# One attention and MLP layer in fp32: four small edits to the pipelined attention stage (a shared store buffer, an earlier weight load, a later place for short score columns, an earlier activation table load)

## The chip, the cores and the metric

The kernel runs on one core of a Trainium2 chip. The metric is the device time of one execution in microseconds (us), lower is better. A time that is shown is the median of several executions; the profile and the trace come from one further execution that the hardware profiler recorded.

Engines are named as the profile names them: PE is TensorE (its matmuls), PEld its weight loads, DVE is VectorE, ACT is ScalarE, POOL is GpSimd, SP is SyncE, which here issues nearly all DMAs. SPq and ACTq are the sequencers of SP and ACT, where their DMAs are issued.

## The reference

The layer has 2048 tokens and width 1024. It is an attention sub-layer and an MLP, each behind an RMS norm with shift, scale and gate from a conditioning vector. The attention has 16 heads of width 64 in two groups of eight.

```python
proj = h @ w_in[l]                          # 1024 -> 3072
q_sb, k_sb, v_sb, q_ca, k_ca, v_ca = jnp.split(proj, split_pts, axis=-1)
# group A, "stick-breaking", strictly causal:
w = jnp.where(strict, jnp.exp(log_beta + suffix), 0.0)   # suffix: cumulative sum of log(1 - beta)
# group B, chunked softmax over the own chunk of 64 and 8 chunks before it, with a relative bias:
p = jax.nn.softmax(s + bias, axis=-1)
mixed = jnp.concatenate([o_sb, o_ca], axis=-1)
x = x + gt1 * (mixed @ w_o[l])
x = x + gt2 * (jnp.square(jax.nn.relu(h2 @ w1[l])) @ w2[l])
```

## The kernel before, in words

Every fp32 product on PE is made of three matmuls on two fp32r halves ("hi" and "lo": `split`, a cast on ACT for hi and a subtraction on DVE or POOL for lo). Helpers record every PE, DVE, ACT and POOL instruction at one line (42), so that the profile's groups are told apart by the names of tiles. Tokens stand reversed, in four blocks of 512 (`TB`).

The program has three stages. Up to about 400 us the first stage projects blocks 3 and 2, and parts of 1 and 0, to queries, keys and values in scratch memory (`scr_q`, `scr_k`, `scr_v`). From about 400 to 1285 us the attention stage runs, which the change touches. From there to the end the MLP runs, and the trace shows it as matmuls `ps`.

**The attention stage** is one loop written out by hand (line 1303) over steps; four steps make a unit. A unit is one head and one block of queries, and for group A (class `SB`, `ca` 0) one block of keys as well; for group B (class `CA`, `ca` 1) it has a window of 640 keys for each 128 queries. Units come in this order: group A for query blocks 2 and 3, group B for 1, 2 and 3, group A for 1 and 0, group B for 0. So there are three turns from one group to the other (`turned`, line 1320). In one step the loop issues, in this order:

- for the unit two units back (`LAG` 8 steps): `transposes`, four PE transposes of finished weights into a PSUM bank `wt`;
- for the unit in front: `soft1` (group A: a sigmoid `z<-z` on ACT, a scan `p` on DVE and differences `b` on POOL; group B: bias added and minimum taken on DVE, `s<-cz` and `s<-ct`). At a turn it comes after the next item;
- `parts`: the split of `wt` into `wth` (ACT) and `wtl` (DVE), which frees its bank;
- `soft2` (group B: the exponential `e<-s` on ACT). At a turn it is the first exponential or sigmoid after the other kind, and ACT first loads a table (ACT_TABLE_LOAD);
- jobs of the step before (`done`): among them the sums and stores of finished heads;
- the value product `acc` of an older unit;
- `scores` for the next step (`z`, and `cz` in group B);
- `fill`: dense matmuls that have nothing to do with this unit, some six of 128x256 or three of 128x512 in a step (line 1344). A credit, which grows with the weight of each step, sets how many.

PE runs its instructions in this written order. The four PSUM banks of tag "z" are shared by `z`, `cz`, `ct` and `wt`; two banks of tag "ps" hold the dense work, and two hold `acc`.

**Short columns.** A row of group B has 640 scores and a bank 512. So 384 are made as `cz`, and the last 256 of two row blocks share one bank, `ct`. `ends(0)` makes it for row blocks 0 and 1 ahead of their first `cz`; `ends(2)` makes it for row blocks 2 and 3 in `scores` of row block 1, right behind that `cz`. DVE reads its part of `ct` one row block ahead (`tail`), behind `s<-cz` of the row block at hand.

**The dense work of the attention stage** is first the rest of the projection (`fill_qkv`, matmuls `pf`) for block 1 and then block 0, cut in pieces of 256 columns. A piece's weights are two halves of 1 MB (`fw`, four of the eight row groups each), in a ring of three buffers. While a piece runs, the halves of the next one are asked for in its second half of columns (`j` 1, line 1097). A piece of queries or keys has one pass over the eight row groups `k` there; a piece of values (4, 5, 10, 11) has two passes (`tt` 0 and 1), and both requests stand in the second: half 0 at `k` 0, and half 1 at `k` 4. Half 1 goes into the buffer of the running piece's half 0, whose last reader is `k` 3 of that second pass. After `fill_qkv` the dense work is the output projection (`outproj`, matmuls `po`, weights `ow`).

**Stores.** A piece's result is cast to `stf` or `svf` from pool `fp` (tag "st", three buffers), split, and stored by SP to `scr_q`, `scr_k` or `scr_v`. The output of two heads (`finish`, `total`, `keep`, lines 788 to 812) is added on POOL as `o`, cast by ACT to the hi half of `os`, subtracted on POOL to the lo half, and stored by SP to `scr_m`. `os` has one buffer of its own in pool `op` (line 806): the next cast to it waits until the store before has landed.

SP issues its DMAs in an order that the framework's scheduler sets; each waits in that queue for its own conditions, and what is behind it waits too.

Of the kernel before, what the change touches and what calls it, by code (L numbers as in the profile page):

```python
# [10 lines left out]
F32R = mybir.dt.float32r  # L11
BF16 = mybir.dt.bfloat16
AF = mybir.ActivationFunctionType
# [5 lines left out]
P = 128  # L19
# [6 lines left out]
TB = 512  # L26
# [53 lines left out]
def encoder_kernel(ctx, tc, xT, x3, wf, c, g1, g2, w_in, w_rest, gqk, bias, w_o, w1, w2, w_ada, b_ada, out):  # L80
    nc = tc.nc
    act, dve, pool, sp = nc.scalar, nc.vector, nc.gpsimd, nc.sync
# [35 lines left out]
    zero = cpool.tile([P, 1], F32, name="zero")  # L118
# [9 lines left out]
    cols = cpool.tile([P, 184], F32, name="cols")  # L128
# [116 lines left out]
    if True:  # L245
# [18 lines left out]
        behind = Later()  # L264
# [238 lines left out]
        act, dve, pool = (Ordered(tc, e) for e in (act, dve, pool))  # L503
# [130 lines left out]
        for k in range(KT):  # L634
            if k + 4 < KT:
                load_first(k + 4)
            j = k + 1
# [112 lines left out]
    ph = ctx.enter_context(ExitStack())  # L750
    if True:
# [51 lines left out]

        def keep(u, o):

            os = op.tile([P, 2, TB], F32R, tag="os", name=f"os{u.nm}", bufs=1)
            split(os[:, 0, :], os[:, 1, :], o, pool)
            q = act if u is units[-1] else sp
            q.dma_start(scr_m[u.g, u.ca * 4 + u.h // 2], os.bitcast(F32))
            pairs[u.g] += 1  # L810
            if pairs[u.g] == KT and u.g > 0:
                filler.append(Filler(outproj, u.g))
# [48 lines left out]
        class SB(Unit):  # L861
# [60 lines left out]
            def soft2(self, qi):  # L922
                pass

            def weights(self, qi, kb):
                w, c0 = self.ws[qi]
                return w[:, kb * P - c0 : (kb + 1) * P - c0]

        class CA(Unit):
# [39 lines left out]
            def scores(self, qi):  # L969
                nm = f"{self.nm}_{qi}"  # L970
                n, hn = self.size(qi)
                if qi == 0 and n > hn:
                    self.ends(0)
                self.z = z = pz.tile([P, TB], F32, tag="z", name=f"cz{nm}")
                ks = slice(qi * P, qi * P + hn)
                for l in range(2):
                    pe.matmul(z[:, :hn], self.q[:, l, qi * P : (qi + 1) * P], self.k[:, ks], start=l == 0, stop=l == 1)
                if qi == 1 and n > hn:
                    self.ends(2)

# [91 lines left out]
        def fill_qkv(self, tb, ht, pieces):  # L1072

            def load(piece, i):
                w = ring.tile([P, KT // 2, 2, CW], F32R, tag="r8", name=f"fw{tb}_{piece}_{i}")
                sp.dma_start(w.bitcast(F32), scr_w[piece,][:, i * 4 : i * 4 + 4, :, :])
                return w

            self.tiles = ht or []
            self.firsts = [lambda i=i: load(pieces[0], i) for i in range(2)]  # L1080
            yield None if ht else lambda k: scr_h[:, k]
            ht = self.moving()
            nxt = self.weights()
            yield "wait" if tb == 0 else "start"
            for n, piece in enumerate(pieces):
                grp, hf = divmod(piece, 2)
                w, nxt = nxt, []
                for j in range(2):
                    if n == len(pieces) - 1 and j:
                        yield "ahead"  # L1090
                    nm = f"f{tb}_{piece}_{j}"
                    ps = dense.tile([P, TB], F32, tag="ps", name=f"p{nm}")
                    last = 0 if grp < 2 else 1
                    for tt in range(last + 1):
                        tl = slice((2 * j + tt) * P, (2 * j + tt + 1) * P)
                        for k in range(KT):
                            if j and tt == last and k in (0, 4):
                                if n + 1 < len(pieces):
                                    nxt.append(load(pieces[n + 1], k // 4))
                                else:  # L1100
                                    yield "weight"
                            wk = w[k // 4][:, k % 4]
                            for i, (a, b) in enumerate(((0, 0), (0, 1), (1, 0))):
                                flags = {"start": k == 0 and i == 0, "stop": k == KT - 1 and i == 2}
                                if grp < 2:
                                    pe.matmul(ps, wk[:, a, j * P : (j + 1) * P], ht[k][:, b, :], **flags)
                                    yield 1.0
                                else:
                                    pe.matmul(ps[:, tt * CW : (tt + 1) * CW], ht[k][:, b, tl], wk[:, a, :], **flags)
                                    yield 0.5  # L1110

                    def keep(grp=grp, hf=hf, j=j, ps=ps, nm=nm, piece=piece):
                        if grp < 2:
                            st = fp.tile([P, 2, TB], F32R, tag="st", name=f"st{nm}")
                            src, hi, lo = ps, st[:, 0, :], st[:, 1, :]
                            home = scr_k[0, tb, hf * 2 + j].rearrange("l d t -> d l t") if grp else scr_q[0, tb, hf * 2 + j]
                        else:
                            st = fp.tile([P, 4, 2, 2, HD], F32R, tag="st", name=f"sv{nm}")
                            src, hi, lo = ps.rearrange("p (t h d) -> p h t d", t=2, d=HD), st[:, :, :, 0, :], st[:, :, :, 1, :]
                            home = scr_v[grp // 3, tb, hf][:, :, 2 * j : 2 * j + 2, :].rearrange("h p t e -> p h (t e)")  # L1120
                        act.copy(hi, src)

                        st2 = st if grp < 2 else st.rearrange("p h t l d -> p h (t l d)")

                        def rest(lo=lo, src=src, hi=hi, home=home, st2=st2, got=(piece, tb) if j else None):
                            dve.tensor_tensor(lo, src, hi.bitcast(F32), op=ALU.subtract)
                            sp.dma_start(home, st2.bitcast(F32))
                            if got:
                                have.add(got)

                        second.append(rest)

                    yield keep
# [146 lines left out]
        def value(u, j):  # L1280
            u.values(j)
# [14 lines left out]
        op = ph.enter_context(tc.tile_pool(name="op", bufs=2))  # L1296
        pado = ph.enter_context(tc.tile_pool(name="pado", bufs=1))
        pado.tile([P, 80], F32, tag="pad", name="pado")
        fp = ph.enter_context(tc.tile_pool(name="fp", bufs=3))
        wtp = ph.enter_context(tc.tile_pool(name="wtp", bufs=4))  # L1300
        ldq = sp
        steps = [(u, st) for u in units for st in range(STEPS)]
        for i in range(len(steps) + LAG):
            if i % STEPS == 0:
                if i // STEPS + AHEAD < len(units):
                    load(units[i // STEPS + AHEAD])
            vi = i - VST
            if vi >= 0 and vi % STEPS == 0 and vi // STEPS < len(units):
                units[vi // STEPS].load_values()
            front, fs = steps[i] if i < len(steps) else (None, 0)  # L1310
            back, bs = steps[i - LAG] if i >= LAG else (None, 0)
            done = list(soon)
            soon.clear()
            js = []
            if back is not None:
                nb = len(back.banks)
                js = range(nb * bs // STEPS, nb * (bs + 1) // STEPS)
            for j in js:
                back.transposes(j)
            turned = front is not None and i and front.ca != steps[i - 1][0].ca  # L1320
            if front is not None and not turned:
                front.soft1(fs)
            while first:
                first.pop(0)()
            while second:
                second.pop(0)()
            for j in js:
                back.parts(j)
                late.append((back, j))
            if turned:  # L1330
                front.soft1(fs)
            if front is not None:
                front.soft2(fs)
            for job in done:
                if turned:
                    later.add(3, job)
                else:
                    job()
            while len(late) > AVLAG:
                value(*late.pop(0))  # L1340
            if i + 1 < len(steps):
                u, st = steps[i + 1]
                u.scores(st)
            fill(front.weight if front else 0.6, 6 if turned else 0)
            later.tick()
        for u, j in late:
            value(u, j)
# [20 lines left out]
    if True:  # L1368
# [34 lines left out]
        steps, jobs = [], {}  # L1403
# [346 lines left out]
        for mb in (1, 0):  # L1750
            begin = len(steps)
            steps += [First(mb, j, i) for j in range(NP) for i in PRODUCTS]
            for j in range(NP):
                f = steps[begin + 7 * j]
# [124 lines left out]
```

## Time and profile before

| what | before |
|---|---|
| median of 3 executions | 2567.85 us (2565.67 to 2570.01) |
| the profiled execution's own time | 2574.0 us |
| span of the profile | 2572.2 us |
| granted TensorE clock, mean | 0.999 |
| PE busy | 2553.0 us, 12851 matmuls |
| weight loads busy (PEld) | 2155.4 us |
| DVE, ACT, POOL busy | 1867.0, 1394.8, 903.1 us |
| moved by DMA | 633.90 MB, mean 246 GB/s |
| ACT_TABLE_LOAD | 4 of 1.28 us |
| `os` casts and stores to `scr_m` | 32 |

PE is the engine that the others feed. Its busy time leaves 19.2 us of the span, start and end included. Matmuls are pipelined and their ends are modelled, so that a stretch that shows PE busy may still hold some slack; the idle times that the trace puts ahead of an instruction, with their releasers, are the safer reading. A wait is named after what ended last. The clock granted to TensorE is given for any stretch: at 1.00 a matmul of 512 columns takes its normal time, at 0.50 twice that.

### The profile page before, as it was taken

The page shows a single profiled execution, that of the slowest core. Times are in us where ns is not written, and L with a number is a line of the kernel's source. Part 1 is how long each engine was busy: PE and PEld are TensorE (multiplying, and loading weights), DVE is VectorE, ACT ScalarE, POOL GpSimd, SP SyncE. Part 2 cuts the span into 40 slices and gives each one's busy share as a digit, 9 for nine tenths or more (in the row PEclk, how much of TensorE's full clock was granted, in tenths as well). Part 3 has the DMA queues.
Part 4 walks back from the last instruction along what each step waited for, and adds up shares of the span by engine and source line. Part 5 has one row for each costly group of instructions (what it writes and reads, how often), then busy time and mean ns, then how long its engine had stood idle before and what let it go on. Part 6 is the DMA issues. An engine that isn't in the chain of part 4 may idle for free.

```text
span 2572.2 us, 39216 instructions
## 1 busy us (share of the span) xinstructions
PE 2553.0 (99%) x12851; PEld 2155.4 (84%) x12851; DVE 1867.0 (73%) x3102; ACT 1394.8 (54%) x2596; POOL 903.1 (35%) x1232
## 2 busy tenths in 40 slices
PE   9999999999999999999999999999999999999999
PEld 7888888888988988888978888888888888888887
DVE  7656767787778899898687777768766655645655
ACT  7323434668886666666754444556444545544443
POOL 4330244667666666666513333000003323100000
PEclk9999999999999999999999999999999999999999
DMA  9879887788887685766787767966764343465574
GB/s 394 341 283 371 316 321 255 227 271 262 251 249 259 210 280 191 241 196 217 233 331 260 268 249 285 329 234 223 254 239 149 140 168 144 157 241 196 200 270 152
DMA packets 251263, 633.90 MB, mean 246 GB/s; under 512 B 28209, under 2 KB 56881, under 8 KB 241202
## 3 DMA queue, kind: packets, MB, share of 16 engines
q1 hardware_dynamic: 249760, 626.67, 70.5%
q10 hardware_dynamic: 1298, 4.72, 0.4%
q8 instruction: 101, 1.65, 0.3%
q14 instruction: 104, 0.85, 0.1%
HBM read 439.92 MB, written 191.37 MB: 245 GB/s over the span
## 4 chain that ended last, share of the span: by engine, by line
PE 91%; DVE 3%; DMA 2%; ACT 2%; issue 1%; POOL 1%; SPq 0%; ACTq 0%; DVEq 0%; POOLq 0%
PE ps L42 47%; PE pt L42 11%; PE acc L42 7%; PE wt L42 6%; PE pf L42 5%; PE z L42 5%; PE po L42 4%; PE pq L42 3%; PE cz L42 2%; PE ct L42 1%; DVE p L42 1%; DMA scr_m<-os 1%; PE px L42 1%; POOL b L42 0%; DVE h L42 0%
## 5 line engine op out<-in xcount | busy, mean ns | idle before, releaser
L42 PE MATMUL ps<-oph,opv 128*128 128x512 f32 x2688 | 611.9, 390 | 0.2
L42 PE MATMUL ps<-h,opw 128*128 128x512 f32 x2664 | 604.2, 389 | 0.0
L42 PEld LDWEIGHTS ps<-oph,opv 128*128 128x128 f32 x2688 | 504.1, 188 | 106.0 <-DVE opv L42 0.8
L42 PEld LDWEIGHTS ps<-h,opw 128*128 128x128 f32 x2664 | 500.3, 188 | 103.6
L42 POOL TENSOR_TENSOR b<-p 128x512 f32<-128x512 f32 (+1 forms) x320 | 292.0, 912 | 207.2 <-DVE p L42 122.4
L42 ACT CAST wth<-wt 128x512 fp32r<-128x512 f32 (+1 forms) x432 | 244.0, 567 | 173.2 <-PE wt L42 169.0
L42 DVE TENSOR_TENSOR wtl<-wt,wth 128x512 fp32r<-128x512 f32 (+1 forms) x432 | 280.4, 653 | 66.8 <-ACT wth L42 65.3
L42 DVE TENSOR_TENSOR oph<-hw,oph 128x512 fp32r<-128x512 f32 x224 | 156.8, 700 | 211.8 <-ACT oph L42 211.8
L42 ACT CAST oph<-hw 128x512 fp32r<-128x512 f32 x224 | 139.3, 622 | 275.4 <-PE ps L42 273.7
L42 PE MATMUL pt<-w,ht 128*128 128x512 f32 x1248 | 288.0, 391 | 0.0
L42 POOL TENSOR_TENSOR ts<-w 128x512 f32<-128x512 f32 x32 | 46.5, 1452 | 660.4 <-DMA w<-in_w_dram 512.2
L42 PEld LDWEIGHTS pt<-w,ht 128*128 128x128 f32 x1248 | 233.1, 188 | 47.4
L42 DVE TENSOR_TENSOR_SCAN p<-z,p,zero 128x512 f32<-128x512 f32 x192 | 245.7, 1281 | 34.4 <-ACT z L42 23.8
L42 PE MATMUL acc<-wth,v 128*128 128x512 f32 (+3 forms) x544 | 218.0, 405 | 0.0
L42 ACT ACTIVATE z<-z 128x512 f32<-128x512 f32 (+1 forms) x320 | 165.9, 520 | 63.6 <-PE z L42 59.6
L42 PE MATMUL z<-k,q 128*128 128x512 f32 (+3 forms) x640 | 184.5, 370 | 2.3 <-DVE p L42 2.0
L42 PE MATMUL acc<-wtl,v 128*128 128x512 f32 (+3 forms) x544 | 181.7, 348 | 0.0
L42 DVE TENSOR_TENSOR opw<-w,opw 128x512 fp32r<-128x512 f32 x127 | 96.9, 765 | 113.2 <-ACT opw L42 113.1
L42 POOL TENSOR_TENSOR e<-e,cols 128x640 f32<-128x640 f32 (+1 forms) x128 | 142.8, 1120 | 86.7 <-DVE cols L42 73.0
L42 PE MATMUL wt<-ident,b 128*128 128x128 f32 x1088 | 166.7, 273 | 3.6 <-DVE p L42 3.0
L42 PE MATMUL po<-fx,ow 128*128 128x512 f32 x576 | 162.0, 393 | 0.0
L42 PEld LDWEIGHTS wt<-ident,b 128*128 128x128 f32 x1088 | 133.1, 141 | 30.7 <-DVE p L42 3.4
(200 smaller groups left out, 4085.5 us busy)
## 6 DMA issues: line engine op xcount, KB each, us to landing
hw<-scr_hid SPq DMA_DIRECT2D x112, 512.0 KB, 3.7
q<-scr_q SPq DMA_DIRECT2D x128, 256.0 KB, 4.5
w<-in_w_dram SPq DMA_DIRECT2D x64, 512.0 KB, 5.4
hw<-scr_s SPq DMA_DIRECT2D x64, 512.0 KB, 4.6
fw<-scr_w SPq DMA_DIRECT2D x28, 1024.0 KB, 6.7
k<-scr_k SPq DMA_DIRECT2D x224, 128.0 KB, 4.0
v<-scr_v SPq DMA_DIRECT2D x112, 256.0 KB, 4.1
wa<-in_w_ada_dram SPq DMA_DIRECT2D x48, 512.0 KB, 7.9
```

Source lines behind the costliest of these rows:

```text
L42: return lambda *x, **y: self.tc.keep_in_program_order(f(*x, **y))
```

## The change

Four edits, all in the attention stage:

1. `keep` takes `os` from pool `fp`, tag "st", which gets four buffers in place of three; the buffer of its own in `op` goes. The memory used is the same. `os`, `stf` and `svf` now take their buffers in turn from one ring.
2. The call `ends(2)` moves from `scores` into a new method `behind`, which the loop calls after `fill`. So the second `ct` of a unit stands behind that step's dense matmuls. Group A has an empty `behind`.
3. In `fill_qkv` half 0 of the next piece's weights is asked for at `k` 0 of the first pass (`tt` 0) and no more of the last; half 1 stays at `k` 4 of the last pass. For pieces of queries and keys, whose only pass is both, nothing changes.
4. At a turn the loop issues a one-column activation (into a column of `cols` that nothing reads) with the function that the front unit will need, ahead of `parts`. ACT's table load so comes ahead of the casts `wth` and no more behind them.

```diff
         def keep(u, o):
 
-            os = op.tile([P, 2, TB], F32R, tag="os", name=f"os{u.nm}", bufs=1)
+            os = fp.tile([P, 2, TB], F32R, tag="st", name=f"os{u.nm}")
             split(os[:, 0, :], os[:, 1, :], o, pool)
...
+            def behind(self, qi):
+                pass
+
...
                     pe.matmul(z[:, :hn], self.q[:, l, qi * P : (qi + 1) * P], self.k[:, ks], start=l == 0, stop=l == 1)
+
+            def behind(self, qi):
+                n, hn = self.size(qi)
                 if qi == 1 and n > hn:
                     self.ends(2)
...
-                            if j and tt == last and k in (0, 4):
+                            if j and (tt, k) in ((0, 0), (last, 4)):
                                 if n + 1 < len(pieces):
                                     nxt.append(load(pieces[n + 1], k // 4))
...
-        fp = ph.enter_context(tc.tile_pool(name="fp", bufs=3))
+        fp = ph.enter_context(tc.tile_pool(name="fp", bufs=4))
...
+            if turned:
+                act.activation(cols[:, 1:2], zero, AF.Exp if front.ca else AF.Sigmoid)
             for j in js:
                 back.parts(j)
...
             fill(front.weight if front else 0.6, 6 if turned else 0)
+            if i + 1 < len(steps):
+                u.behind(st)
             later.tick()
```

What moves is shown at three places. The first is SP's queue in the dense work of block 0, between pieces 4 and 5 of the values. `fw_5_1` is half 1 of piece 5, `fw_10_0` half 0 of piece 10, `svf_4_1` a result of piece 4, and `xr` are rows of the input. Before:

```order
L236 DMA xr_2_11577<-in_xT_dram 128x512
L778 DMA k_2_1_2_9819<-scr_k_2_1_117 64x512 x2
L785 DMA v_2_1_2_10087<-scr_v_2_0_144 128x512
L1076 DMA fw_5_1_9813<-scr_w_225 128x2048
L1076 DMA fw_10_0_10215<-scr_w_230 128x2048
L778 DMA k_2_1_3_9920<-scr_k_3_1_121 64x512
L1127 DMA scr_v_0_0_140<-svf_4_1_9876 128x4x256
```

After:

```order
L236 DMA xr_2_11579<-in_xT_dram 128x512
L778 DMA k_2_1_2_9821<-scr_k_2_1_117 64x512 x2
L785 DMA v_2_1_2_10089<-scr_v_2_0_144 128x512
L1082 DMA fw_5_1_9815<-scr_w_225 128x2048
L1082 DMA fw_10_0_10137<-scr_w_230 128x2048
L778 DMA k_2_1_3_9922<-scr_k_3_1_121 64x512
L1133 DMA scr_v_0_0_140<-svf_4_1_9878 128x4x256
```

Nothing moved here: `fw_10_0` is asked for sooner in the program (the last number in a name counts up with the program's order, 10215 and 10137), and stands at the same place in the queue. Elsewhere half 0 of piece 11 of block 1, of piece 2 of block 1 and of piece 11 of block 0 moved ahead by one to three rows of SP's queue.

The second is PE at the third turn, in the first unit of group B for query block 0 (head 0). `cz_0_0_1` are the scores of row block 1, `ct_0_0_2` the short columns of row blocks 2 and 3, and `po` the dense work. Before:

```order
L42 MATMUL cz_0_0_1_15145<-k_0_0_14895,q_0_0_14892 128x384 x2
L42 MATMUL ct_0_0_2_15148<-k_0_0_14895,q_0_0_14892 128x256 x4
L42 MATMUL po_0_15081<-fx_3_14829,ow_0_14564 128x512 x3
L42 MATMUL po_0_15081<-fx_4_15043,ow_0_14564 128x512 x3
L42 MATMUL po_0_15081<-fx_5_15045,ow_0_14564 128x512 x3
L42 MATMUL wt_7_0_2_1_15162<-ident,b_7_0_2_0_14902 128x128
```

After:

```order
L42 MATMUL cz_0_0_1_15147<-k_0_0_14897,q_0_0_14894 128x384 x2
L42 MATMUL po_0_15083<-fx_3_14831,ow_0_14566 128x512 x3
L42 MATMUL po_0_15083<-fx_4_15045,ow_0_14566 128x512 x3
L42 MATMUL po_0_15083<-fx_5_15047,ow_0_14566 128x512 x3
L42 MATMUL ct_0_0_2_15160<-k_0_0_14897,q_0_0_14894 128x256 x4
L42 MATMUL wt_7_0_2_1_15165<-ident,b_7_0_2_0_14904 128x128
```

`ct_0_0_2` moved behind nine dense matmuls. In 22 of the 24 units of group B it moved so, most often behind three; in two (head 0 of block 1, at the first turn, and head 1 of block 0) no dense matmul stands in that step and nothing moved.

The third is ACT at the first turn, from group A to B. `wth_7_2_2_2` and `wth_7_2_3_0` are casts of two steps, and `e_0_1_0` is the first exponential. Before:

```order
L42 ACTIVATE z_7_3_3_3_6264<-z_7_3_3_3_6264 128x128
L42 CAST wth_7_2_2_2_6278<-wt_7_2_2_2_6269 128x256
L42 CAST wth_7_2_3_0_6302<-wt_7_2_3_0_6297 128x512
L42 ACT_TABLE_LOAD
L42 ACTIVATE e_0_1_0_6311,cols<-s_0_1_0_6306,cols 128x640
```

After:

```order
L42 ACTIVATE z_7_3_3_3_6264<-z_7_3_3_3_6264 128x128
L42 CAST wth_7_2_2_2_6278<-wt_7_2_2_2_6269 128x256
L42 ACT_TABLE_LOAD
L42 ACTIVATE cols<-zero 128x1
L42 CAST wth_7_2_3_0_6303<-wt_7_2_3_0_6297 128x512
L42 ACTIVATE e_0_1_0_6312,cols<-s_0_1_0_6307,cols 128x640
```

The load and a one-column activation moved ahead of the cast; the other two turns change in the same way. On DVE and POOL no instruction moved.

## Prediction

> **What bounds the kernel now.** I read the page's totals first, then PE's own waits in the attention stage (400 to 1285 us), and then the timeline around the longest of them. The page says how little there is to win.
>
> ```profile
> span 2572.2 us, 39216 instructions
> ...
> PE 2553.0 (99%) x12851; PEld 2155.4 (84%) x12851; DVE 1867.0 (73%) x3102; ACT 1394.8 (54%) x2596; POOL 903.1 (35%) x1232
> ```
>
> PE is busy in all but 19.2 us. No edit takes a matmul away, so the change can return only what PE waits, and what its clock loses behind a wait. PE's waits in the attention stage, with total, count and longest:
>
> ```profile
> PE wt L42 <- DVE p L42: 3.0, 1, 3.0
> PE pf L42 <- DMA fw<-scr_w: 2.2, 1, 2.2
> PE z L42 <- DVE p L42: 2.0, 6, 0.6
> PE ct L42 <- DVE wtl L42: 1.3, 2, 0.6
> PE wt L42 <- DVE cols L42: 0.3, 1, 0.3
> PE wt L42 <- DVE wtl L42: 0.2, 1, 0.2
> PE ct L42 <- DVE cols L42: 0.2, 1, 0.2
> ```
>
> They sum to 9.2 us, and two single waits hold most. I call them A (3.0) and B (2.2), and the change speaks to both.
>
> **Wait A, edit 1.** The chain of waits has one store in it, shown from its issue to its landing:
>
> ```profile
> 462.94 8.29 DMA scr_m<-os
> ```
>
> The view of the line that issues these stores gives all 31 that SP issues:
>
> ```profile
> DMA to landing us min/median/max: 2.6/3.0/8.3
> ```
>
> ACT's, DVE's and PE's rows there (start, duration, and at the end the idle time before, with its releaser):
>
> ```profile
> 471.31 0.62 ACT L42 CAST os<-o 128x512 fp32r<-128x512 f32 x1 [4.52 <-DMA scr_m<-os]
> 471.83 0.58 ACT L42 CAST svf<-pf 128x512 fp32r<-128x512 f32 x1
> 472.31 1.07 ACT L42 ACTIVATE z<-z 128x512 f32<-128x512 f32 x2
> ```
>
> ```profile
> 473.00 1.28 DVE L42 TENSOR_TENSOR_SCAN p<-z,p,zero 128x512 f32<-128x512 f32 x1 [5.50 <-ACT z L42]
> ```
>
> ```profile
> 470.52 0.84 PE L42 MATMUL pf<-ht,fw 128*128 128x512 f32 x3
> 474.34 0.66 PE L42 MATMUL wt<-ident,b 128*128 128x128 f32 x4 [2.98 <-DVE p L42]
> ...
> 476.11 1.22 PE L42 MATMUL z<-k,q 128*128 128x512 f32 x2 [0.65 <-DVE p L42]
> ```
>
> The second of two `os` casts finds the only buffer still in flight to memory. ACT stands for 4.52 us, and the sigmoids `z` queue behind it; DVE's scan comes late, and PE waits for the bank that the scan frees: 2.98, then 0.65 us. The clock falls behind it, and behind B as well (window, then busy time of PE, PEld, DVE, ACT, POOL, then granted clock, DMA share, GB/s):
>
> ```profile
> 476.40:479.80 3.40, 3.40 (x10) 2.68 (x10) 3.40 (x5) 0.95 (x2) 2.19 (x5) 0.54 0.86 258
> 810.90:814.30 3.40, 3.40 (x16) 3.31 (x15) 1.65 (x2) 2.15 (x5) 0.14 (x1) 0.54 0.72 220
> ```
>
> At 0.54 for 3.40 us, 0.46 x 3.40 = 1.6 us of PE's work are lost. A costs 2.98 + 0.65 + 1.6 = 5.2 us.
>
> With a ring of four the cast needs only `o`, which POOL ends about 467.06:
>
> ```profile
> 465.77 1.29 POOL L42 TENSOR_TENSOR o<-o,otmp 128x512 f32<-128x512 f32 x1
> ```
>
> It starts at 467.1 in place of 471.31, 4.2 us sooner, and so do the `svf` cast, the sigmoids and the scan. PE's bank is then free at 474.34 - 4.2 = 470.1, while PE comes to it at 471.36 (470.52 + 0.84): 1.2 us to spare, so the whole stall goes. What is late next there are weights: half 1 of the running piece, 1 MB. It was issued ahead of that store in the same queue, so that I put its landing no later than the store's, 462.94 + 8.29 = 471.23; PE wants it in its next step, behind a `wt`, an `acc` and a `z`, about 1 us after 471.36 (an estimate). I take -5.2. The bound on the other side, if that cover fails, is 0.
>
> [...] Wait B stopped PE for 2.20 us, and the clock stood at 0.54 afterwards. [...]
>
> **Wait B, edit 3: 0.** The chain shows one weight transfer, and PE the place where it was missed:
>
> ```profile
> 800.13 9.34 DMA fw<-scr_w
> ```
>
> ```profile
> 804.58 1.34 PE L42 MATMUL pf<-fw,fx 128*128 128x256 f32 x10
> ...
> 806.91 0.40 PE L42 MATMUL pf<-fw,fx 128*128 128x256 f32 x2
> 809.51 0.73 PE L42 MATMUL pf<-fw,fx 128*128 128x256 f32 x4 [2.20 <-DMA fw<-scr_w]
> ```
>
> Ten and two matmuls are the twelve of `k` 0 to 3 (three each), which use half 0 of piece 5. The next uses half 1, `fw_5_1`. That half is asked for at `k` 4 before and after, because its buffer is free only when `k` 3 of piece 4 has been read; the edit asks sooner for half 0 alone, which was in time. In SP's queue `fw_5_1` and `fw_10_0` stand where they stood, with the same conditions. So B stays, 2.20 + 1.6 = 3.8 us, and the edit gives 0. The three rows of `fw` that do move in SP's queue are issued ahead of query, value and `scr_m` transfers, none of which is a releaser in PE's waits above; bounds 0 and one more wait like B, +3.8, and I take 0, as the list of waits has it.
>
> **Short columns, edit 2.** `ct` waited twice for `wtl` and once for `cols` (rows above), first here, at the first turn:
>
> ```profile
> 567.93 0.74 PE L42 MATMUL ct<-k,q 128*128 128x256 f32 x4 [0.64 <-DVE wtl L42]
> ```
>
> At this turn nothing moves, and 0.64 stays. The other, 1.3 - 0.6 = 0.7, is at the third turn; nine dense matmuls now stand ahead of it there; three of them take 0.86 us (next rows), so nine outlast the wait, and it goes. With the 0.2 at a moved `ct`, -0.9. Against it, DVE reads `ct` later. A plain step of group B shows how much it bears:
>
> ```profile
> 601.18 0.65 PE L42 MATMUL ct<-k,q 128*128 128x256 f32 x4
> 601.67 0.86 PE L42 MATMUL pf<-ht,fw 128*128 128x512 f32 x3
> ```
>
> ```profile
> 602.26 0.42 DVE L42 CUSTOM_DVE_ANT_0 s<-ct,bias 128x256 f32<-128x256 f32 x1
> ...
> 603.67 0.69 DVE L42 TENSOR_TENSOR wtl<-wt,wth 128x512 fp32r<-128x512 f32 x1 [0.91 <-ACT wth L42]
> ```
>
> `ct` ends at 601.83. The pair ends at 602.53 in either order, so that `ct` behind the three dense ones ends 0.70 later. DVE, which reads it at 602.26, comes 0.27 late; `wtl` had 0.91 idle ahead of it: covered.
>
> **Tables, edit 4.** A turn's rows on ACT, first turn and second:
>
> ```profile
> 566.57 0.59 ACT L42 CAST wth<-wt 128x512 fp32r<-128x512 f32 x1 [1.60 <-PE wt L42]
> 568.96 1.28 ACT L42 ACT_TABLE_LOAD   x1 [1.80 <-DVE cols L42]
> ```
>
> ```profile
> 762.24 0.58 ACT L42 CAST wth<-wt 128x512 fp32r<-128x512 f32 x1
> 762.84 1.28 ACT L42 ACT_TABLE_LOAD   x1
> 764.13 0.97 ACT L42 ACTIVATE z<-z 128x512 f32<-128x512 f32 x2
> ```
>
> The nearest row for the new one-column activation, from the groups of ACT (busy time, mean ns):
>
> ```profile
> L42 ACT ACTIVATE aff<-mod,gcol 128x1 f32<-128x1 f32 x8 | 3.1, 386 | 5.6 <-DVE mod L42 5.6
> ```
>
> Its cost lies between 0 and that 0.39. At the first turn ACT has 1.60 us free ahead of the cast, and load and activation take 1.28 to 1.67: they fit but for 0.07 us, the exponential comes 1.28 sooner, and PE was not waiting for it: 0. At the second there is no wait ahead of the cast: it moves by up to 1.67 us and the sigmoids by up to 0.39, while the six extra dense matmuls that a turn is given cover PE. Bounds 0 and +0.4; I take +0.2. The third is like the first: 0.
>
> [...]
>
> **Sum.** -5.2 - 0.9 + 0.2 + 0 = -5.9 us, from 2574.0 for the profiled execution to 2568.1. That execution is 6.15 above the median of the runs, 2567.85, and 4.0 above the slowest. I apply the difference to the median: **2562.0**. A measurement of this kernel can tell about 0.2% from no change, here 5.1 us (2562.7), so the forecast lies just beyond it.
>
> **The rivals.**
>
> *The store is quicker in timed runs.* A needs a landing over 8.29 - 3.6 = 4.7 us after the issue, and the median is 3.0. That timed runs are 4 to 8 us faster than the profiled one speaks for it; that the store is issued behind 1 MB of weights in the same queue, in every execution, against. Gain 0.7: 2567.2. Chance 0.15, no change.
>
> *Both waits go.* If edit 3 reaches B after all (less traffic beside `fw_5_1`), -5.9 - 3.8 = -9.7: 2558.2. The unmoved rows speak against; B's margin of only 2.2 us, for. Chance 0.13, faster.
>
> *The clock falls anyway.* The half clock has another cause than PE's gaps: -5.9 + 1.6 = -4.3, 2563.6. Both falls stand right behind the two longest gaps, which speaks against. Chance 0.07, no change.
>
> *Late short columns hold DVE.* In group B, at 22 places, if DVE's read of `ct` comes over 0.91 us late, `wtl` is late, the bank is not free, and PE waits up to the 0.70 by which `ct` moved: 22 x 0.70 = 15.4. With A gone and no gain on `ct`: -5.2 + 0.2 + 15.4 = +10.4, 2578.3; it ends slower from 0.46 us a place on. The 0.27 worked out above speaks against. Chance 0.08, slower.
>
> *The shared ring makes casts wait.* A cast of `stf` or `os` waits when the store four buffers back has not landed: 5.2 us a time by A's price. It takes three to end slower (-5.9 + 15.6 = +9.7, 2577.5). Against it: the longest landing of `os` is 8.3 us, and four more casts would have to come within it, where the stretch at A shows two. Chance 0.05, slower.
>
> **How the numbers follow.** The forecast has 0.52; its own range is 2559.6 to 2565.3 (-6.1 to -4.8 by the bounds of edits 2 and 4, and the 2.2 us by which the timed runs lie around their median), with 0.33 of it beyond 2562.7. Faster: 0.33 + 0.13 = 0.46. Same: 0.19 + 0.15 + 0.07 = 0.41. Slower: 0.13. The range reaches from 2558.2 - 2.2 = 2556.0 to 2567.2 + 2.2 = 2569.4; the slower cases are left out.
>
> **What would show it.** Right: no ACT wait of `os` on a store; the clock at 1.00 around 470 to 480; PE's wait for `fw` still there near 800, with its half clock; `ct` waits of 0.6 in all, at the first turn alone; three table loads ahead of casts. Wrong: a gap of PE near 470 all the same, B gone, `wtl` or `ct` with a wait in many steps of group B, or `stf` and `os` waiting for stores.

## The result, and the profile after

| | before | after |
|---|---|---|
| median of 22 executions each, in turns on one chip | 2569.94 us (2563.97 to 2577.32) | 2564.64 us (2562.45 to 2568.85) |
| ratio after to before | | 0.9985, 95% interval 0.9978 to 0.9991 |
| the profiled execution, its span | 2574.0, 2572.2 us | 2562.64, 2560.9 us |
| granted TensorE clock, mean | 0.999 | 1.000 |

The change is faster by 0.15% (0.09 to 0.22%), that is 3.9 us (2.3 to 5.7). The forecast was 5.9 us. The medians lie 5.3 us apart. The gain is under the 0.2% (5.1 us) that the prediction took as the least that can be told from no change; with 22 executions each the interval still leaves out 1.

The profiled executions lie 11.4 us apart, twice as far as the medians. The page of after:

```profile
span 2560.9 us, 39227 instructions
...
PE 2548.6 (100%) x12851; PEld 2153.9 (84%) x12851; DVE 1866.3 (73%) x3102; ACT 1396.2 (55%) x2599; POOL 903.4 (35%) x1232
```

PE's waits in the attention stage of after (400 to 1285 us; total, count, longest):

```profile
PE z L42 <- DVE p L42: 1.7, 5, 0.6
PE ct L42 <- DVE wtl L42: 0.6, 1, 0.6
PE wt L42 <- DVE cols L42: 0.3, 1, 0.3
PE wt L42 <- DVE wtl L42: 0.2, 1, 0.2
```

PE's idle time fell from 19.2 to 12.3 us, and its busy time by 4.4 us, of which 3.2 are, by the prediction's estimate, the two half clocks of before. The waits sum to 2.8 us where before had 9.2. A is gone, `ct` waits at the first turn alone, and **B is gone too**, against the forecast.

The place of A on ACT in after, and the landings of all `os` stores that SP issues:

```profile
467.40 0.62 ACT L42 CAST os<-o 128x512 fp32r<-128x512 f32 x1 [0.31 <-POOL o L42]
467.92 0.58 ACT L42 CAST svf<-pf 128x512 fp32r<-128x512 f32 x1
468.40 1.07 ACT L42 ACTIVATE z<-z 128x512 f32<-128x512 f32 x2
...
DMA to landing us min/median/max: 2.6/2.9/6.8
```

The cast waits for POOL's `o` alone. It starts 4.15 us after the first store was issued (463.25); the forecast had 467.1 against 462.94, 4.16 us. The store still took 6.8 us to land, and nobody waits for it. The windows there (window, busy time of PE, PEld, DVE, ACT, POOL, clock, DMA share, GB/s) show PE full and the clock at 1.00:

```profile
469.90:473.30 3.40, 3.40 (x19) 2.84 (x18) 3.40 (x5) 1.98 (x4) 2.40 (x5) 1.00 0.75 281
473.30:476.70 3.40, 3.40 (x20) 2.83 (x19) 3.40 (x5) 2.48 (x6) 2.19 (x5) 1.00 0.99 291
```

At the first turn ACT has the table load ahead of the cast:

```profile
559.35 0.38 ACT L42 CAST wth<-wt 128x256 fp32r<-128x256 f32 x1 [0.53 <-PE wt L42]
559.74 1.28 ACT L42 ACT_TABLE_LOAD   x1
561.03 0.20 ACT L42 ACTIVATE cols<-zero 128x1 f32<-128x1 f32 x1
561.31 0.59 ACT L42 CAST wth<-wt 128x512 fp32r<-128x512 f32 x1
563.72 0.83 ACT L42 ACTIVATE e<-s,cols 128x640 f32<-128x640 f32 x1 [1.82 <-DVE cols L42]
```

The one-column activation took 0.20 us (forecast 0 to 0.39). The exponential starts as soon as DVE's columns are there, with no load in between, and PE, which was not waiting for it, gains nothing, as forecast. At the place of B, half 1 of piece 5 landed sooner than in before (9.3); its issue in after (count, size, us to landing):

```profile
fw<-scr_w SPq DMA_DIRECT2D x1, 1024.0 KB, 6.9
```

SP issues the same rows around it at the same distances in both traces (`fw` 1.05 us behind `v` in each, and 5.37 and 5.34 us behind `scr_m`), so no edit had moved this transfer. That was the open question, together with the size: which edit gave the 3.9 us, and what took B away?

### The profile page after: what moved, and what is told of

It is laid out like the page before. It is cut to its first block, busy times and chain, and to the rows that moved or that the text cites. A ratio compares the mean times of both kernels' runs of the same rounds, so it can differ in the third digit from the quotient of the medians.

```text
span 2560.9 us, 39227 instructions
## 1 busy us (share of the span) xinstructions
PE 2548.6 (100%) x12851; PEld 2153.9 (84%) x12851; DVE 1866.3 (73%) x3102; ACT 1396.2 (55%) x2599; POOL 903.4 (35%) x1232
## 4 chain that ended last, share of the span: by engine, by line
PE 92%; DVE 3%; ACT 1%; DMA 1%; issue 1%; POOL 1%; SPq 0%; DVEq 0%; ACTq 0%; POOLq 0%
PE ps L42 46%; PE pt L42 11%; PE acc L42 7%; PE wt L42 7%; PE pf L42 6%; PE z L42 5%; PE po L42 4%; PE pq L42 3%; PE cz L42 2%; PE ct L42 1%; DVE p L42 1%; DVE h L42 1%; PE px L42 1%; POOL b L42 0%; DVE cy L42 0%
## 5 line engine op out<-in xcount | busy, mean ns | idle before, releaser
L42 DVE TENSOR_TENSOR opv<-hw,opv 128x512 fp32r<-128x512 f32 x224 | 155.8, 695 | 0.0
```

Source lines behind the costliest of these rows:

```text
L42: return lambda *x, **y: self.tc.keep_in_program_order(f(*x, **y))
```

## The experiments

Each was timed in turns with the kernel before, whose executions the kernels of one group share. Every edit not named is as in the kernel it starts from. The last column counts executions of 2568 us and more; I chose that limit after seeing the runs, because those of before fall into two heaps there (their medians are 2566.05 and 2570.55).

| kernel | edits in | median us | ratio to before, 95% | at or over 2568 |
|---|---|---|---|---|
| before, four groups together | none | | | 54 of 116 |
| after | 1, 2, 3, 4 | 2564.64 | 0.9985 (0.9978 to 0.9991) | 2 of 22 |
| e1_ring | 1 | 2565.28 | 0.9993 (0.9984 to 1.0001) | 1 of 11 |
| e2_ct | 2 | 2567.95 | 0.9995 (0.9985 to 1.0005) | 4 of 11 |
| e3_weights | 3 | 2567.59 | 1.0000 (0.9990 to 1.0009) | 5 of 11 |
| e4_table | 4 | 2566.50 | 1.0001 (0.9991 to 1.0010) | 4 of 12 |
| store_first | none, two DMAs exchanged | 2565.30 | 0.9989 (0.9980 to 0.9997) | 0 of 11 |
| heavy_before | none, more stored | 2569.42 | 1.0009 (0.9997 to 1.0021) | 10 of 12 |
| heavy_after | all, more stored | 2563.40 | 0.9983 (0.9972 to 0.9993) | 0 of 12 |
| ring3 | all, ring of 3 | 2564.06 | 0.9985 (0.9976 to 0.9994) | 1 of 11 |
| late6 | all, half 1 asked later | 2562.82 | 0.9983 (0.9973 to 0.9992) | 0 of 10 |
| halves | all, other order of `k` | 2563.51 | 0.9984 (0.9976 to 0.9993) | 2 of 11 |
| late_order | all, other order of `k` | 2563.96 | 0.9985 (0.9974 to 0.9996) | 0 of 10 |

### Each edit alone

The parts of the diff are those of the change. Edit 1 (e1_ring):

> Edit 1 alone (os in a ring of four with the other stores; weights, ct and tables as before). My theory, the store is what ACT waits for: no row of ACT waits for scr_m<-os, PE has no gap near 470 us and the clock stands at 1.00 there; the time falls by 3 to 5.2 us (a ratio of 0.9980 to 0.9988), nearly all that the whole change gave. PE's ct waits stay at 1.3 to 1.5 us. PE's wait for fw near 800 is there only when that half of the weights lands later than 7.2 us after its issue (9.34 less the 2.20 that PE waited). Rival, the store is quick in timed runs: at most -0.7 us, a ratio of 0.9997 or more, and the gain of the whole change comes from another edit.

ACT's cast near A, and the landing of the store before it (issued at 464.55):

```profile
468.71 0.62 ACT L42 CAST os<-o 128x512 fp32r<-128x512 f32 x1 [0.31 <-POOL o L42]
...
scr_m<-os SPq DMA_DIRECT2D x1, 512.0 KB, 8.7
```

The store was as late as in before (8.7 against 8.3 us), and the wait is gone all the same. The time fell by 2.8 us by the medians and 1.8 by the ratio, with an interval that reaches zero: less than forecast. Ten of eleven executions are under 2568 us.

Edit 2 (e2_ct):

> Edit 2 alone (the second pair of short columns behind the dense matmuls). My theory: PE's ct waits go from 1.5 us in all to 0.6 at the first turn alone; the time falls by 0 to 0.9 us, a ratio of 0.9996 to 1.0000. ACT's wait for the os store and PE's gap near 470 are there if that store lands later than 4.7 us. Rival, the late ct holds DVE: up to 0.70 us at 22 places, +15.4 us and a ratio of 1.006, with PE waits behind wtl in many steps between 570 and 760 us.

```profile
PE ct L42 <- DVE wtl L42: 0.6, 1, 0.6
```

That is the whole of PE's waits at `ct`, 0.6 us at the first turn, as forecast. No wait behind `wtl` came up in group B. The ratio is close to the 0.9996 that 0.9 us would give, and cannot be told from 1. This kernel has the single `os` buffer, and in its trace A is missing too. Its cast, and the landing of the store before it:

```profile
468.79 0.62 ACT L42 CAST os<-o 128x512 fp32r<-128x512 f32 x1 [0.71 <-DMA scr_m<-os]
...
scr_m<-os SPq DMA_DIRECT2D x1, 512.0 KB, 4.5
```

ACT waits 0.71 us, and PE does not stop: 4.5 is under the 4.7 us that the forecast put as A's threshold. So A comes and goes with the execution.

Edit 3 (e3_weights):

> Edit 3 alone (half 0 of the next piece asked for sooner, in values pieces). My theory: the half that PE missed near 800 us is half 1 of the next piece, which is not moved; whether PE waits there is decided by its landing in that execution (over or under 7.2 us), so that the time is as before within 0.7 us, a ratio of 0.9995 to 1.0005, and the os wait stays. Rival, the edit clears the traffic beside that half: the half lands under 7.2 us every time and 3.8 us come back, a ratio of 0.9985.

The ratio is 1.0000. Neither A (the store landed in 4.5 us) nor B is in its trace, yet 5 of 11 executions are over 2568 us. The rival's 0.9985 lies outside the interval. The timing alone could not show whether the edit reaches B, for B turned out to be rare (below); but it is missing as well in the traces of e1_ring, e2_ct and heavy_before, which do not have this edit.

Edit 4 (e4_table):

> Edit 4 alone (a one-column activation ahead of the casts at the three turns). My theory: the table load stands ahead of the cast, where ACT waits for PE's transposes; PE's wait for ct at the first turn stays at 0.6 us; the time is as before, 0 to +0.4 us, a ratio of 1.0000 to 1.0002. [...]

The ratio is 1.0001, and PE's `ct` wait at the first turn stayed 0.6 us. In the rows of after above the load takes its 1.28 us and no more: cast until 559.73, load from 559.74, activation at 561.03. The profiled execution of this kernel was the longest of all, 2579.95 us, and shows A and B again. Its waits, and the two transfers in the chain:

```profile
PE pf L42 <- DMA fw<-scr_w: 3.3, 1, 3.3
PE wt L42 <- DVE p L42: 3.0, 1, 3.0
...
463.26 8.38 DMA scr_m<-os
801.60 10.36 DMA fw<-scr_w
```

### What makes A: the store's place, the buffer, the dose

**store_first** exchanges the first `os` store and the 1 MB ahead of it in SP's queue, in the kernel before (`osp` keeps the program's order):

```diff
-            q = act if u is units[-1] else sp
+            q = act if u is units[-1] else osp if (u.ca, u.g, u.h) == (0, 2, 1) else sp
...
-                sp.dma_start(w.bitcast(F32), scr_w[piece,][:, i * 4 : i * 4 + 4, :, :])
+                (osp if (tb, piece, i) == (1, 2, 1) else sp).dma_start(w.bitcast(F32), scr_w[piece,][:, i * 4 : i * 4 + 4, :, :])
```

> The kernel before with one exchange in SP's queue: the first os store (462.94 in the trace of before) is issued ahead of the 1 MB of weights that stood before it; no edit of the change. My theory, wait A is that one store queued behind the weights, and it comes in about half of the executions: the store lands within 4.7 us of its issue, ACT's os wait and PE's gap near 470 are gone, and the runs at 2568 us and more thin out, as with edit 1 alone: the median falls by 2 to 5 us, a ratio of 0.998 to 0.9993. The weights are asked for 2.3 us later; PE needs them about 9.4 us after that, so that a wait of up to 1 us may come. Rival, the store is late by itself (its own transfer, whatever is ahead of it): its landing stays at 8 us in the executions that are slow, A stays, a ratio of 0.9995 to 1.0005.

The landing of that store in its trace:

```profile
scr_m<-os SPq DMA_DIRECT2D x1, 512.0 KB, 3.0
```

No cast waits for it, PE waits nowhere for the weights that now come behind it (its one wait for `fw`, 0.16 us, is at B's place, 802.55), and none of 11 executions reaches 2568 us. With none of the four edits, the time falls by 0.11% (0.03 to 0.20%). So A is that one store behind those weights.

**heavy_before** and **heavy_after** put two more copies of the same `os` ahead of the store:

```diff
+            if (u.ca, u.g, u.h) == (0, 2, 1):
+                for x in range(2):
+                    sp.dma_start(scr_e[x], os.bitcast(F32))
             q.dma_start(scr_m[u.g, u.ca * 4 + u.h // 2], os.bitcast(F32))
```

> The kernel before with the first os store doubled twice: two more copies of the same os (512 KB each) are written to memory ahead of the store itself, and the one os buffer is free when all three have landed; the copies are extra work that nothing reads. My theory, A is the landing of that store over 4.7 us, and comes in those executions in which it is late: 1 MB more takes 2.7 us at the 389 GB/s seen there, so that the landing is 7.7 to 11 us and A comes in every execution: a gap of PE near 470 of 3.0 to 6.3 us with a half clock of 1.6 to 3.2 behind it, no run under 2567 us, the median 3 to 7 us over that of before, a ratio of 1.001 to 1.003. Rival, ACT's wait only follows something else that is late in some executions: A in half of them as before, a ratio under 1.001.

> The changed kernel with the same two more copies of the first os store. My theory, with a ring of four no cast needs that buffer back so soon: no os wait, no gap near 470, the time of the changed kernel within 1 us, a ratio to before of 0.998 to 0.9990. Rival, the extra traffic itself (queries, keys and weights behind it in the queue) makes PE wait: 2 us or more at q, k or fw, in the list of waits, and a ratio of 0.9993 or more.

ACT and PE in heavy_before (the three copies were issued from 464.35 on):

```profile
471.32 0.62 ACT L42 CAST os<-o 128x512 fp32r<-128x512 f32 x1 [3.11 <-DMA scr_m<-os]
...
474.36 0.66 PE L42 MATMUL wt<-ident,b 128*128 128x128 f32 x4 [1.58 <-DVE p L42]
...
476.13 0.73 PE L42 MATMUL z<-k,q 128*128 128x512 f32 x2 [0.65 <-DVE p L42]
```

The buffer came free 6.97 us after the first issue (471.32 - 464.35). PE lost 1.58 + 0.65 = 2.23 us, and 6.97 - 4.7 is 2.27: the threshold holds at a second dose. No execution is under 2567.49 us, where 15 of the 29 of before in this group are. The slowdown of 2.1 us by the medians is under the 3 to 7 expected, since I had put the landing too long; the expected half clock did not come either (the granted clock of that execution is 1.000 in the mean, and one half clock of 3.41 us takes 1.7 us of 2567.0, which would give 0.999). The interval reaches zero, and the ratio by itself, 1.0009, is as the rival has it; what speaks against the rival is the spread: 10 of 12 executions at or over 2568 us, where before has 11 of 29 in this group. heavy_after stores the same copies, waits for none of them and is as fast as after; the intervals of the two do not meet.

**ring3** gives the ring three buffers in place of four:

```diff
-        fp = ph.enter_context(tc.tile_pool(name="fp", bufs=4))
+        fp = ph.enter_context(tc.tile_pool(name="fp", bufs=3))
```

> The changed kernel with a ring of three buffers in place of four for the stores, os among them. My theory, the ring needs one buffer for each store that can be on its way at one time, and at wait A these are os, svf and os: three are enough, the time is that of the changed kernel within 1 us, a ratio to before of 0.998 to 0.9990. Rival, a shared ring makes the casts of os, stf and svf wait for stores two or three back: ACT waits on scr_m, scr_v, scr_q or scr_k, at up to 5.2 us of PE's time each, a ratio of 1.000 or more.

The cast behind a store that took 8.1 us to land:

```profile
468.75 0.62 ACT L42 CAST os<-o 128x512 fp32r<-128x512 f32 x1 [0.32 <-POOL o L42]
...
scr_m<-os SPq DMA_DIRECT2D x1, 512.0 KB, 8.1
```

No cast of the attention stage waits for a store, and the time is that of after. Three buffers in common do what one apart and three could not, and the rival of a ring that makes casts wait falls.

### What makes B

**late6** asks for half 1 two `k` later in the program:

```diff
-                            if j and (tt, k) in ((0, 0), (last, 4)):
+                            if j and (tt, k) in ((0, 0), (last, 6)):
...
-                                    nxt.append(load(pieces[n + 1], k // 4))
+                                    nxt.append(load(pieces[n + 1], min(k, 1)))
```

> The changed kernel, but half 1 of the next piece is asked for two k later (at k 6 in place of k 4). My theory, B is the landing of that half against 8 k of dense work, about 0.9 us each in a values piece: with 6 k there are 5.4 us, less than the 6.9 to 9.4 us of the landings seen, so that PE waits 1.5 to 4 us at each of the four changes from one values piece to another, in every execution: +6 to +16 us on the changed kernel, and half clocks behind the longer waits. Rival, other traffic and not the time of asking makes B: PE waits at the same one place, near 800, or nowhere, and the time is that of the changed kernel within 2 us.

**late_order** lets the last block read half 0 last:

```diff
-                        for k in range(KT):
+                        ks = (4, 5, 6, 7, 0, 1, 2, 3) if j and tt and grp > 1 else range(KT)
+                        for k in ks:
```

> The changed kernel with the k of the last block of a values piece in the order 4 to 7, 0 to 3, so that half 0 of the running piece is read to the end of the piece and its buffer, in which half 1 of the next piece lands, is free 4 k later. The time left for the landing is then 4 k of the next piece, 3.6 us, in place of 8 k, 7.2 us. My theory, B is that landing against that time: PE waits for fw at each change from a values piece to another (four of them), 1.5 to 6 us each, in every execution, in all 6 to 24 us, and up to four half clocks of 1.6 us: a ratio to before of 1.001 to 1.010. Rival, B is a disturbance near 800 alone: PE waits at one place or none, a ratio of 0.9985.

Both expectations were wrong, and both for the same reason: neither edit moved the transfer. SP's issue and the dense matmuls beside it, late6 first, then after:

```profile
793.71 0.75 PE L42 MATMUL pf<-fw,fx 128*128 128x256 f32 x5
...
794.02 3.57 SPq L1082 DMA_DIRECT2D fw<-scr_w  x2
```

```profile
794.25 0.74 PE L42 MATMUL pf<-fw,fx 128*128 128x256 f32 x5
...
794.55 3.57 SPq L1082 DMA_DIRECT2D fw<-scr_w  x2
```

In both it is issued 0.3 us after the same matmul starts, as in late_order (795.60 after 795.29). Here SP issues when a buffer comes free, not when the program's text asks. So the times, which are as the two rivals have them, do not tell the theory from the rivals. In late_order the matmul it waits for, the twelfth of the last block's 24, reads half 1 and not half 0, so that the load seems to take whichever buffer is free first; I infer that, no row names the buffer. late_order did give one more measured wait for B, with the landing of its transfer:

```profile
795.60 7.53 DMA fw<-scr_w
...
803.17 0.74 PE L42 MATMUL pf<-fw,fx 128*128 128x256 f32 x4 [0.42 <-DMA fw<-scr_w]
```

Landing less wait is 9.34 - 2.20 = 7.14 in before, 10.36 - 3.26 = 7.10 in e4_table and 7.53 - 0.42 = 7.11 here. The 0.16 us of store_first, with a landing of 7.3, and 0.15 us in the trace of gaps (below), with 7.2, agree. With 6.9 in after there was none. B is a landing over 7.1 us.

**halves** moves that threshold: a values piece does `k` 0 to 3 for both blocks, then 4 to 7 for both, so that a buffer comes free sooner and half 1 is needed later.

```diff
-                    for tt in range(last + 1):
-                        tl = slice((2 * j + tt) * P, (2 * j + tt + 1) * P)
-                        for k in range(KT):
-                            if j and (tt, k) in ((0, 0), (last, 4)):
+                    for half in range(2):
+                        for tt, k in product(range(last + 1), range(half * 4, half * 4 + 4)):
+                            tl = slice((2 * j + tt) * P, (2 * j + tt + 1) * P)
+                            if j and (tt, k) in ((0, 0), (0, 4)):
```

> The changed kernel, with the matmuls of a values piece ordered by halves of k (k 0 to 3 for both blocks of rows, then k 4 to 7 for both), so that half 0 of the running piece comes free after 8 of 16 k in place of 12, half 1 of the next is asked for then, and is needed after 8 k of the next in place of 4: 16 k, some 14 us, for a landing of at most 10.4 us seen. My theory: PE never waits for fw, in any execution; the median is 0 to 3 us under that of the changed kernel, a ratio to before of 0.9970 to 0.9985. Rival, B is not what is left in the slower runs: the median is that of the changed kernel, a ratio of 0.9985, with the same spread of runs.

Its transfer:

```profile
fw<-scr_w SPq DMA_DIRECT2D x1, 1024.0 KB, 8.9
```

A landing of 8.9 us is 1.8 over the old threshold, and PE did not wait for `fw`. So the cure of B works in this execution; the timed gain does not show it (0.9984 against 0.9985, the rival's number), and with B this rare it could hardly do so: of 13 traces with the old threshold, two have it over 0.5 us. That PE never waits for `fw` in any execution, as expected, is not shown by one trace, and 2 of 11 executions are at or over 2568 us.

### The clock behind a stop

**gaps** makes PE stand twelve times in the MLP, for chains of POOL operations:

```diff
+                if j == 0 and i != 1:
+                    for _ in range(GAPS[mb, i]):
+                        pool.tensor_tensor(cols[:, 0:100], cols[:, 0:100], ones[:, 0:100], op=ALU.mult)
+                    pe.matmul(Second.banks[i][0][:, 0:1], ident, cols[:, 0:1], start=True, stop=True)
```

> The changed kernel with twelve stops of PE in the second half of the MLP: ahead of a product's first matmul PE waits for a chain of 0 to 9 small POOL operations behind the last result of the product before it (extra work, with no use). The stops are some 1 to 5 us long, by the length of the chain, and some 40 us apart; the time is 25 to 60 us over the changed kernel. My theory from B (a stop of 2.2 us, then 3.4 us at half clock): the granted clock falls to 0.5 for 3.4 us behind the stops of about 2.2 us and more, and stays at 1.00 behind those under 1.5 us. [...]

It took 2663.74 us, 99 over after where 25 to 60 were expected, in one execution. PE waited eleven times for these chains, 65.1 us in all and 9.6 at the longest, more than planned. The granted clock is 0.982 in the mean, so that about 96 us ran at half clock (2 x 0.018 x 2662.0, an estimate). A stop of 2.36 us, and the windows of 3.41 us around it on the grid that the falls keep:

```profile
2402.24 0.38 PE L42 MATMUL ps<-cols,ident 128*128 128x1 f32 x2 [2.36 <-POOL cols L42]
...
2400.06:2403.48 3.42, 1.24 (x6) 1.08 (x7) 2.68 (x5) 0.99 (x2) 0.58 (x1) 1.00 0.10 38
2403.48:2406.89 3.41, 3.41 (x9) 2.67 (x8) 0.00 (x0) 0.00 (x0) 0.00 (x0) 0.50 0.90 296
```

A stop of 2.36 us, and the clock stands at 0.50 for the next 3.41 us, as the theory has it. But that the length decides falls by B in e4_table, a longer stop:

```profile
812.00 0.74 PE L42 MATMUL pf<-fw,fx 128*128 128x256 f32 x4 [3.26 <-DMA fw<-scr_w]
```

Windows of 3.41 us around it, on the grid of that trace, with the clock at 1.00 in the one behind:

```profile
806.92:810.34 3.42, 1.82 (x12) 1.45 (x11) 3.42 (x5) 0.95 (x2) 2.22 (x4) 1.00 0.78 315
810.34:813.75 3.41, 1.75 (x12) 1.66 (x13) 0.12 (x1) 0.48 (x1) 1.16 (x2) 1.00 1.03 311
813.75:817.16 3.41, 3.41 (x30) 3.41 (x29) 2.32 (x4) 2.77 (x7) 0.50 (x1) 1.00 0.68 150
```

The stop lay across the edge of two windows, PE was busy for half of each (1.82 and 1.75 us of 3.41), and no fall followed.

## Why the prediction was right or wrong

**Wait A, edit 1: mechanism, place and price right, the frequency missing.** The step that failed is the one by which I kept the rival of a quicker store at 0.15: "that the store is issued behind 1 MB of weights in the same queue, in every execution". The order in the queue is the same in every execution; the landing is not. With the weights just ahead of it the store landed in 4.3 to 4.5 us in three traces (e2_ct, e3_weights, late6) and in 6.8 to 8.7 in seven, and the threshold of 4.7 lies between. The price of 5.2 us agrees with the heaps of before: their medians lie 4.5 us apart, their means 5.0. But only 54 of 116 executions are in the upper heap. That this heap is A's is an inference from the counts, since few executions were traced: at or over 2568 us are 13 of 34 executions of the single edits that leave A in (2, 3 and 4), and 6 of 98 of the eight kernels without it. With 54 of 116, A costs about 0.47 x 5.0 = 2.3 us on average. That is what edit 1 alone (1.8) and store_first (2.8) gave, within their intervals. A profile of one execution had shown me one heap of two.

**Wait B, edit 3: the edit gives 0, right; "So B stays", wrong.** B is no property of the order but of a landing over 7.1 us, and the trace of before is one of the two that had it. The edit is not what took it away: the transfer stands where it stood, and B is missing in traces without the edit too. Both traces with a wait of ACT over 4 us at A also have B, and none of the others has B over 0.5 us; whether the one brings the other is not settled. That the heaps lie some 5 us apart, and not the 9 us of both prices, speaks against its doing so each time.

**Short columns, edit 2: right in the trace, too small to time.** The waits went from 1.5 to 0.6 us, and DVE's later reading made PE wait nowhere.

**Tables, edit 4: 0 to +0.4 us, in keeping with 1.0001 (0.9991 to 1.0010).**

**The sum.** With A at 2.3 in place of 5.2, edit 2's 0.9 and edit 4's 0.2 the forecast would have been -3.0 us, and measured are -3.9 (-5.7 to -2.3). The -5.9 is just outside. Subtracting the whole of A from a median that holds it in half of the executions was the mistake; that the profiled execution stood 6.15 us above the median, which I noted, was its sign. That the measured time fell inside the forecast's own range (a gain of 2.55 to 8.25 us) does not bear the -5.9 out, for -3.0 lies in that range too.

**What is left.** After still has executions of 2567 to 2569 us. A third stop of PE, at the first MLP product (around 1335 us), is 3.42 us in e1_ring, 3.0 in e4_table and 3.2 in gaps, and at most 1.4 in the other traces. In e1_ring and gaps the profile names nothing that PE waited for there. No edit touches it, and I did not try to remove it.

## What to carry to other kernels

A wait on a DMA in one trace is a sample (here one store landed in 4.3 to 8.7 us behind the same weights): before its price goes into a sum, look at how the timed runs spread, and work out the landing time from which the wait begins. A buffer that must be home again within a few microseconds (4.7 here) was safer in a ring shared with other stores than alone, at the same memory (1 of 11 executions of e1_ring at or over 2568 us, 54 of 116 of before); where there is no room, exchange the store with a large load ahead of it (0 of 11 in store_first). When a load is moved in the program's text, check in the trace that its issue moved, for what sets it may be the buffer (in after, late6 and late_order it came 0.3 us after the start of a matmul, wherever the text asked).

## What the runs showed of the hardware

**The late store's landing has a tail in which few DMA engines work.** Windows of before behind the issue of the late store:

```profile
466.00:468.00 2.00, 2.00 (x10) 1.64 (x10) 1.51 (x3) 0.59 (x1) 1.92 (x4) 1.00 0.98 294
468.00:469.00 1.00, 1.00 (x6) 0.82 (x5) 0.00 (x0) 0.00 (x0) 0.41 (x2) 1.00 0.30 76
469.00:471.20 2.20, 2.20 (x13) 1.64 (x11) 0.00 (x0) 0.00 (x0) 0.00 (x0) 1.00 0.06 26
```

Up to 468 the mean busy share of the 16 DMA engines is 0.98. Then it falls to 0.30 and to 0.06, the work of about five engines and of one (16 x 0.30 = 4.8, 16 x 0.06 = 1.0, an estimate), the latter for the last 2.2 us before the landing at 471.23. In e3_weights the store, issued at 463.21, landed in 4.5 us, at 467.7, and up to there the share does not fall:

```profile
467.00:467.80 0.80, 0.80 (x5) 0.66 (x4) 0.78 (x2) 0.10 (x2) 0.72 (x3) 1.00 1.06 302
```

So most of A's extra 3.8 us (8.3 - 4.5), the 3.2 us from 468 to 471.2, is a tail of one to a few DMA engines. In e4_table, whose store landed after 8.38 us, the share falls in the same way, to 0.29 from 468.3 and 0.07 from 469.3. Why they are late in some executions the traces do not say.

**The falls of the clock keep a grid.** In before the two half clocks of the attention stage, 476.10 to 479.52 and 810.61 to 814.03, are 3.413 us long in the trace's clock records, and their starts lie 334.51 us apart, 98 times that; counted from the first clock record they start after 138 and 236 times that. In e1_ring 1338.78 to 1342.19 stood at 0.50. Over the windows shown, and those at A, B and the third stop (PE busy in before 2.08, then 1.13, then the fall; 1.21, then the fall; in e1_ring 1.72, then 0.98, then the fall), a fall came after 0.98, 1.13, 1.21 and 1.24 us busy of 3.41, and none directly after 1.72, 1.75, 1.82 and 2.08. So about 2.2 us of standing within one window were enough (3.41 - 1.21 in before, 3.42 - 1.24 in gaps), and 3.26 us over two were not. What the clock does between 1.24 and 1.72 us busy these rows do not show. What a half clock costs is seen on PE in before: three `pf` matmuls of 128x512 took 1.48 us at 0.50 (477.13) and 0.85 at 1.00 (480.08).
